# Modulation sums of a two-layer diffusion trunk: 32x32 turns and row sums on VectorE in place of the wide sums and transposes on TensorE

## The chip, the core and the metric

The kernel runs on one core of one Trainium2 chip. The metric is the device time of one execution in microseconds (us), from the first instruction to the last. Every engine has its own in-order instruction queue: TensorE (PE, with its weight loads shown apart as PEld), VectorE (DVE), ScalarE (ACT), GpSimd (POOL) and SyncE (SP, which here only starts transfers). Engines wait for each other through semaphores.

## The reference, cut to what matters

Two layers, each of a SwiGLU FFN, a mixing sub-layer and a second FFN, run on a latent stream `x` and a context stream `h` of 256 tokens with 1024 channels each. Every sub-layer is shifted, scaled and gated by nine vectors of 1024 values for each stream that come from a matrix-vector product. These are the modulation vectors, and they are what the change is about:

```python
sc, scc = silu(c), silu(c_ctx)                       # (1, 1024), (1024,)
for l in range(2):
    mod_x = (sc  @ w_mod[l] + b_mod[l]).reshape(b_, 9, 1, 1024)   # w_mod[l]: 1024 x 9216
    mod_h = (scc @ w_mod[l] + b_mod[l]).reshape(9, 1, 1024)
    # sub-layer j uses mod 3j (shift), 3j+1 (scale), 3j+2 (gate)
    y = rmsnorm(s, norm_pre[l, j]) * (1 + scale) + shift
    s = s + weight * gate * rmsnorm(f(y), norm_post[l, j])
```

`f` is `(silu(y @ wg) * (y @ wu)) @ wd` with 2816 hidden columns for the FFNs, and a mix of gated position mixing and two kinds of attention for the middle sub-layer. All of it is float32.

## The kernel before, in words

**Main work.** Every large product is computed in float32 as three products of split numbers: a weight chunk `stg` that a transfer has landed is split into `hi` (ScalarE, line 240) and `lo` (VectorE, line 101), activations are held as `Yh`/`Yl` (and `Uh`/`Ul` for hidden values), and TensorE adds `hi*Yh`, `hi*Yl` (line 250) and `lo*Yh` (line 254). In the FFN a *pair* is two hidden tiles of 128 columns, each with a gate tile `g` and an up tile `u` of 24 matmuls of 512 columns. After each tile, `hidden` makes the SwiGLU on ScalarE and VectorE (lines 566 to 570 and 101). The `down` part uses lines 263, 269 and 271. Weight chunks pass through three `stg` buffers and three `hi` and three `lo` buffers.

**Modulation vectors.** The first two (layer 0, `q` 0 and 1) are computed at the start on TensorE by `mod_first`. The other 16 are computed by `mod_half`, one half of 512 columns at a time: 32 halves in all. A half loads two weight chunks into the same `stg` buffers, and VectorE multiplies them by the per-partition values of `silu(c)` and `silu(c_ctx)` and adds into two accumulators `acc` (one for each stream, 128x512): 2 instructions on line 355 and 14 on line 357. What is left is the sum over the 128 partitions. After a delay `T_MOD` TensorE does it with a matrix of ones (line 367): four matmuls of 256 columns, each for a quarter of the two streams' values, side by side in four groups of 32 columns of the array.

**What follows the sums.** Of the 16 vectors, 6 are gates (`q % 3 == 2`, 12 halves): VectorE adds the bias and multiplies by the norm gain (lines 375 and 376, tiles `gr` of 128x256, for which `by_groups` loads bias and gain by broadcasts on SP's queue), and POOL's queue stores four rows to the table `gtab` in device memory. The other 10 (20 halves) must end with channels on partitions: ScalarE copies the sums to `modev` (line 383), and at the next sum `flip_now` runs the stored `turn`: two 128x128 transposes on TensorE (line 388) and `mod_put` on VectorE (lines 331 to 334), which writes `coef`.

**What sets the order.** The kernel is written by a small planner: `tick(n)` moves a planned clock by `n` TensorE columns, and generators (`task`, `later`) resume when their planned time has come. `step()` starts a half, at most one in `MOD_PACE` us of the planned clock; `drain` forces what is still pending before a vector is used. In practice one half runs with each pair in the FFNs of both layers except the last. `half(...)` takes one of six buffers of 128x512, `pc()` one of two PSUM banks. The instructions of each engine are then placed in a fixed order, which the order listings below show.

Of the kernel before, what the change touches and what calls it, by code (L numbers as in the profile page):

```python
# [12 lines left out]
F32 = mybir.dt.float32  # L13
F32R = mybir.dt.float32r
AF = mybir.ActivationFunctionType
ALU = mybir.AluOpType
# [3 lines left out]
P = 128  # L20
# [15 lines left out]


T_SOFT, T_SOFTC, T_TURN, T_POST = 4.5, 3.5, 1.5, 3.0
T_MOD, T_FLIP, MOD_PACE = 15.0, 2.5, 18.0
PACE_IN, PACE_OUT, PACE_DRAIN = 1.8, 1.0, 1.0  # L40
PACE_IN1, PACE_OUT1, PACE_DRAIN1, T_CHAIN, T_LATE = 1.5, 1.2, 1.2, 7.5, 10.5
PHASES = ((0, 6), (6, 8), (14, 8))
# [21 lines left out]
def trunk(ctx: ExitStack, tc: tile.TileContext, x, c, cx, c_ctx, w_mod, b_mod, norm_pre, norm_post,  # L64
# [16 lines left out]
    def nm(s):  # L81
        cnt[0] += 1
        return f"{s}{cnt[0]}"
# [7 lines left out]
    def pc():  # L91
        return psc.tile([P, 512], F32, tag="c", name=nm("pc"))

    def half(s):
        return wk.tile([P, 512], F32, tag="p", name=nm(s), bufs=6)
# [24 lines left out]
    def tick(n):  # L120
        clk[0] += n / 2400.0
        while evq and not busy[0] and evq[0][0] <= clk[0]:
            run_next()
# [7 lines left out]

        later(delay, run())

    flips = []

    def flip_now():
        while flips:
            flips.pop(0)()

    def drain(tag):  # L140
        while pending.get(tag, 0):
            run_next()
        if tag[0] == "m":
            flip_now()


    ident = const.tile([P, P], F32, name="ident")
    make_identity(nc, ident)
    ones = const.tile([P, P], F32, name="ones")
    nc.vector.memset(ones, 1.0)  # L150
    negh = const.tile([P, 8], F32, name="negh")
    nc.vector.memset(negh, -0.5)
    mask = const.tile([P, 2, P], F32, name="mask")
# [182 lines left out]


    def by_groups(src):
        r = wk.tile([P, 256], F32, tag="sq", name=nm("gr"), bufs=7)
        for j in range(4):  # L340
            nc.sync.dma_start(r[32 * j:32 * j + 32, :],
                              src[256 * (j % 2):256 * (j % 2) + 256].partition_broadcast(32))
        return r

    def mod_half(l, q, hf):
# [15 lines left out]
        if gate:  # L361
            br = by_groups(b_mod[l, c0:c0 + 512])
            gr = by_groups(norm_post[l, j, hf * 512:(hf + 1) * 512])
        yield T_MOD
        t = pc()
        for i in range(4):
            nc.tensor.matmul(t[32 * i:32 * i + 32, 0:256], lhsT=ones[:, 0:32],
                             rhs=acc[i // 2][:, 256 * (i % 2):256 * (i % 2) + 256],
                             start=True, stop=True, tile_position=(0, 32 * i))
        tick(1024)  # L370
        flip_now()
        if gate:

            w = math.sqrt(D) * (1.0 if j == 1 else 0.5)
            nc.vector.tensor_tensor(br, t[:, 0:256], br, op=ALU.add)
            nc.vector.scalar_tensor_tensor(br, br, w, gr, op0=ALU.mult, op1=ALU.mult)  # L376
            for i in range(4):
                f0 = hf * 512 + 256 * (i % 2)
                nc.gpsimd.dma_start(gtab[l, j][i // 2:i // 2 + 1, f0:f0 + 256],  # L379
                                    br[32 * i:32 * i + 1, :])  # L380
            return
        ev = wk.tile([P, 256], F32, tag="sq", name=nm("modev"), bufs=7)
        nc.scalar.activation(ev, t[:, 0:256], AF.Copy)

        def turn():
            u = pc()
            for i in range(2):
                nc.tensor.transpose(u[:, i * P:(i + 1) * P], ev[:, i * P:(i + 1) * P], ident)
            tick(600)
            uv = u[:, 0:256].rearrange("p (i s h r) -> p h i s r", i=2, s=2, h=2)  # L390
            tmp = sm.tile([P, 2, 2, 2], F32, tag="modt", name=nm("modt"))
            for h in range(2):
                mod_put(l, q, 4 * hf + 2 * h, 2, uv[:, h, :, :, 0], tmp[:, h])

        flips.append(turn)

    modq = []

# [930 lines left out]
```

## Time and profile before

| | |
|---|---|
| median of 3 runs | 1762.75 us (1761.02 to 1763.5) |
| the profiled execution's own time | 1762.98 us |
| its span in the trace | 1761.2 us |
| PE busy | 1722.4 us (98%) |
| PEld busy | 1449.9 us (82%) |
| DVE busy | 1190.4 us (68%) |
| ACT busy | 696.3 us (40%) |
| POOL busy | 168.9 us (10%) |
| TensorE clock granted, mean | 0.997 of full speed |

A matmul's record overlaps the next one's, so the duration of one matmul is not what it costs in a full stream: that is the distance from one start to the next. For VectorE and ScalarE, too, the distance of starts is somewhat shorter than a record's duration. Idle time is printed in brackets behind a row, with the engine that ended it.

### The profile page before, as it was taken

Reading aid. Unit: us, or ns where it says so; the run is one execution under the profiler, and the core shown is the slowest. Engines: PE = TensorE matmul, PEld = TensorE weight load, DVE = VectorE, ACT = ScalarE, POOL = GpSimd, SP = SyncE. Lnnn points to the kernel's source line nnn. Section 1 sums busy time; section 2 is a strip of 40 time slices with the busy share of each in tenths; the row PEclk is TensorE's granted clock in tenths of the full one; section 3 lists DMA queues with packets and bytes.
Section 4 is the critical chain, followed back from the end, with each engine's and each line's share of the span. In section 5 each row is a group of like instructions: output and inputs, shape, how many; then the busy total and the mean of one; then the engine's idle time right before and its main releaser. Section 6 shows DMA issues by size and latency. Waiting matters only on the chain.

```text
span 1761.2 us, 24837 instructions
## 1 busy us (share of the span) xinstructions
PE 1722.4 (98%) x9663; PEld 1449.9 (82%) x9663; DVE 1190.4 (68%) x2174; ACT 696.3 (40%) x1480; POOL 168.9 (10%) x185
## 2 busy tenths in 40 slices
PE   7999999999999999999999999999999999999998
PEld 5788888879977789888888898888888897689997
DVE  4876876775667576768766576777864756765555
ACT  4332322244376562333232442332223526655443
POOL 0000000021322120000000210000001321010000
PEclk9999999999999999999999999999999999999999
DMA  9654554543131143445545233655544133226552
GB/s 336 207 173 160 188 197 144 167 150 109 60 103 52 57 137 125 162 163 189 191 144 185 75 120 123 205 178 191 180 144 167 48 108 120 73 90 197 192 191 84
DMA packets 197105, 259.20 MB, mean 147 GB/s; under 512 B 8234, under 2 KB 132348, under 8 KB 196988
## 3 DMA queue, kind: packets, MB, share of 16 engines
q1 hardware_dynamic: 195452, 257.56, 44.3%
q8 instruction: 76, 1.25, 0.3%
q14 instruction: 41, 0.34, 0.1%
q0 software_dynamic: 1536, 0.05, 0.0%
HBM read 256.49 MB, written 1.10 MB: 146 GB/s over the span
## 4 chain that ended last, share of the span: by engine, by line
PE 63%; DVE 7%; ACT 2%; issue 2%; POOL 1%; DMA 1%; POOLq 0%; DVEq 0%; ACTq 0%
PE pa L250 19%; PE pa L254 9%; PE pb L269 4%; PE pb L271 4%; PE pb L263 4%; PE pa L263 4%; PE pa L271 4%; PE pa L269 4%; PE pb L250 3%; DVE lo L101 2%; PE pb L254 1%; PE pa L797 1%; PE pc L818 1%; PE pc L895 1%; DVE S L439 1%
## 5 line engine op out<-in xcount | busy, mean ns | idle before, releaser
L101 DVE TENSOR_TENSOR lo<-stg,hi 128x512 fp32r<-128x512 f32 (+3 forms) x476 | 367.0, 807 | 192.5 <-ACT hi L240 122.8
L240 ACT ACTIVATE hi<-stg 128x512 fp32r<-128x512 f32 (+3 forms) x496 | 318.4, 702 | 329.6 <-PE pa L263 97.2
L250 PE MATMUL pa<-Yh,hi 128*128 128x512 f32 (+1 forms) x1168 | 415.0, 365 | 0.0
L250 PE MATMUL pa<-Yl,hi 128*128 128x512 f32 (+1 forms) x1168 | 413.8, 364 | 0.0
L357 DVE SCALAR_TENSOR_TENSOR acc<-stg,sT,acc 128x512 f32<-128x512 f32 x448 | 305.2, 743 | 4.0 <-DMA stg<-in_w_mod_dram 4.0
L254 PE MATMUL pa<-Yh,lo 128*128 128x512 f32 (+1 forms) x1168 | 257.8, 363 | 0.0
L250 PEld LDWEIGHTS pa<-Yh,hi 128*128 128x128 f32 x1168 | 220.5, 189 | 36.6 <-issue 2.9
L250 PEld LDWEIGHTS pa<-Yl,hi 128*128 128x128 f32 x1168 | 220.5, 189 | 35.0 <-issue 1.2
L254 PEld LDWEIGHTS pa<-Yh,lo 128*128 128x128 f32 x1168 | 202.4, 189 | 34.3
L570 ACT ACTIVATE Uh<-ha 128x512 fp32r<-128x512 f32 (+1 forms) x92 | 50.7, 551 | 296.4 <-DVE ha L568 296.4
L263 PE MATMUL pb<-hi,Ul 128*128 128x512 f32 x400 | 156.9, 392 | 0.0
L271 PE MATMUL pb<-lo,Uh 128*128 128x512 f32 x400 | 155.9, 390 | 0.8 <-DVE lo L101 0.8
L269 PE MATMUL pb<-hi,Uh 128*128 128x512 f32 x400 | 155.8, 391 | 0.1
L568 DVE TENSOR_TENSOR ha<-ha,pa 128x512 f32<-128x512 f32 (+1 forms) x91 | 53.0, 583 | 79.5 <-PE pa L254 79.0
L269 PE MATMUL pa<-Yh,hi 128*128 128x256 f32 x368 | 92.0, 285 | 0.0
L271 PE MATMUL pa<-Yl,hi 128*128 128x256 f32 x368 | 91.3, 283 | 0.0
L271 PEld LDWEIGHTS pb<-lo,Uh 128*128 128x128 f32 x400 | 75.1, 188 | 16.6 <-DVE lo L101 1.3
L263 PEld LDWEIGHTS pb<-hi,Ul 128*128 128x128 f32 x400 | 75.1, 188 | 16.5 <-issue 1.2
L269 PEld LDWEIGHTS pb<-hi,Uh 128*128 128x128 f32 x400 | 75.2, 188 | 16.0 <-DVE Z L503 0.5
L566 ACT ACTIVATE ht<-pa 128x512 f32<-128x512 f32 (+1 forms) x91 | 46.3, 510 | 104.1 <-PE pa L254 81.8
L379 POOL DMA_DIRECT2D gate<-gr x48 | 24.3, 513 | 603.7 <-DVE gr L376 535.3
L567 DVE SCALAR_TENSOR_TENSOR ha<-ht,pa 128x512 f32<-128x512 f32 (+1 forms) x91 | 52.9, 581 | 37.2 <-ACT ht L566 36.4
(299 smaller groups left out, 2732.4 us busy)
## 6 DMA issues: line engine op xcount, KB each, us to landing
stg<-in_w_mod_dram SPq DMA_DIRECT2D x64, 1024.0 KB, 5.0
stg<-in_ffn_w_gate_dram SPq DMA_DIRECT2D x42, 1024.0 KB, 5.2
stg<-in_ffn_w_up_dram SPq DMA_DIRECT2D x42, 1024.0 KB, 5.1
stg<-in_ffn_w_down_dram SPq DMA_DIRECT2D x32, 1024.0 KB, 5.0
stg<-in_w_in_dram SPq DMA_DIRECT2D x14, 1024.0 KB, 4.8
stg<-in_ffn_w_down_dram SPq DMA_DIRECT2D x16, 768.0 KB, 4.4
mst<-in_w_mod_dram SPq DMA_DIRECT2D x16, 512.0 KB, 7.6
stg<-in_w_out_dram SPq DMA_DIRECT2D x8, 1024.0 KB, 6.4
```

The costliest lines, as they stand in the source:

```text
L101: eng.tensor_tensor(lo, full, f32(hi), op=ALU.subtract)
L240: nc.scalar.activation(hi[:, a:b, :], v[:, a:b, :], AF.Copy)
L250: nc.tensor.matmul(o, lhsT=ah, rhs=r, start=(i == 0), stop=(i == n - 1))
L254: nc.tensor.matmul(o, lhsT=al, rhs=bh, start=(i == 0), stop=(i == n - 1))
L263: nc.tensor.matmul(o, lhsT=al, rhs=bh, start=False, stop=last, skip_group_check=True)
L269: nc.tensor.matmul(o, lhsT=ah, rhs=bh, start=(first and k == 0), stop=False, skip_group_check=True)
L271: nc.tensor.matmul(o, lhsT=ah, rhs=bl, start=False, stop=False, skip_group_check=True)
L357: nc.vector.scalar_tensor_tensor(a, v[:, k, :], sc, a, op0=ALU.mult, op1=ALU.add)
L566: nc.scalar.activation(t, g, AF.Tanh, scale=0.5)
L567: nc.vector.scalar_tensor_tensor(a, t, 1.0, g, op0=ALU.add, op1=ALU.mult)
L568: nc.vector.tensor_tensor(a, a, u, op=ALU.mult)
L570: nc.scalar.activation(uh, a, AF.Copy)
```

## The change

1. VectorE gets four new instructions in each half, right behind the products: for each stream a turn of every 32x32 block of `acc` (into a buffer `mt` from `half`) and a sum over each group of 32 along the row, into `sums` (128 x 2 x 16). After that each value is left as four partial sums on four groups of 32 partitions.
2. TensorE adds the four: for a gate with one matmul of 32 columns (`sums` as weights, the selector `sel` as moving data), otherwise with four matmuls of 8 columns in the four column groups (`sel` as weights), whose result already has channels on partitions. The wide sums with `ones`, the ScalarE copy `modev`, the two transposes and the `flips` list go. `mod_put` runs once for 4 blocks and not twice for 2.
3. `by_groups` loads bias and gain into 32x32 tiles (two loads each, not four broadcasts, from a pool of 4 buffers), and a gate's table is stored by two transfers and not four.
4. `T_MOD` goes from 15 to 17, `MOD_PACE` from 18 to 17.5, and the planned clock moves by 600 columns at a sum (before 1024, and 600 at a flip).

```diff
-T_MOD, T_FLIP, MOD_PACE = 15.0, 2.5, 18.0
+T_MOD, T_FLIP, MOD_PACE = 17.0, 2.5, 17.5
...
-    ones = const.tile([P, P], F32, name="ones")
-    nc.vector.memset(ones, 1.0)
+    sel = const.tile([P, 32], F32, name="sel")
+    nc.vector.tensor_reduce(sel, ident.rearrange("p (g j) -> p j g", g=4), axis=AX.X, op=ALU.add)
...
     def by_groups(src):
-        r = wk.tile([P, 256], F32, tag="sq", name=nm("gr"), bufs=7)
-        for j in range(4):
-            nc.sync.dma_start(r[32 * j:32 * j + 32, :],
-                              src[256 * (j % 2):256 * (j % 2) + 256].partition_broadcast(32))
+        r = sm.tile([32, 32], F32, tag="gr", name=nm("gr"))
+        for st in range(2):
+            nc.sync.dma_start(r[16 * st:16 * st + 16, :], src.rearrange("(b c) -> b c", c=32))
...
+        sums = sm.tile([P, 2, 16], F32, tag="sums", name=nm("sums"))
+        for st, a in enumerate(acc):
+            turned = half("mt")
+            nc.vector.transpose(turned, a)
+            nc.vector.tensor_reduce(sums[:, st, :], turned.rearrange("p (b i) -> p b i", i=32), axis=AX.X,
+                                    op=ALU.add)
         yield T_MOD
         t = pc()
-        for i in range(4):
-            nc.tensor.matmul(t[32 * i:32 * i + 32, 0:256], lhsT=ones[:, 0:32],
-                             rhs=acc[i // 2][:, 256 * (i % 2):256 * (i % 2) + 256],
-                             start=True, stop=True, tile_position=(0, 32 * i))
-        tick(1024)
-        flip_now()
         if gate:
+            nc.tensor.matmul(t[0:32, 0:32], lhsT=sums.rearrange("p s b -> p (s b)"), rhs=sel,
+                             start=True, stop=True)
+            tick(600)
...
-        ev = wk.tile([P, 256], F32, tag="sq", name=nm("modev"), bufs=7)
-        nc.scalar.activation(ev, t[:, 0:256], AF.Copy)
-        def turn():
-            u = pc()
-            for i in range(2):
-                nc.tensor.transpose(u[:, i * P:(i + 1) * P], ev[:, i * P:(i + 1) * P], ident)
...
+        sv = sums.rearrange("p s (b m) -> p s b m", m=4)
+        for m in range(4):
+            nc.tensor.matmul(t[32 * m:32 * m + 32, 0:8], lhsT=sel, rhs=sv[:, :, :, m], start=True,
+                             stop=True, tile_position=(0, 32 * m))
+        tick(600)
+        tmp = sm.tile([P, 4, 2], F32, tag="modt4", name=nm("modt"))
+        mod_put(l, q, 4 * hf, 4, t[:, 0:8].rearrange("p (s b) -> p b s", s=2), tmp)
```

**Where the instructions stand now.** First TensorE, in the second phase of the first FFN, at the sum of a half that is not a gate. In the first listing (before) the sum stands between the gate tile and the up tile of a pair, with the flip of the half ahead behind it:

```order
L254 MATMUL pa210_1554<-Yh_102,lo197_1454 128x512 x8
L367 MATMUL pc211_1579<-acc202_1477,ones_89 32x256 x2
L367 MATMUL pc211_1579<-acc203_1478,ones_89 32x256 x2
L388 MATMUL pc212_1584<-ident_84,modev190_1417 128x128 x2
L250 MATMUL pa215_1592<-Yh_102,hi199_1465 128x512
```

The same place in the changed kernel:

```order
L243 MATMUL pa224_1590<-Yh_102,hi209_1469 128x512
L243 MATMUL pa224_1590<-Yl_103,hi209_1469 128x512
L243 MATMUL pa224_1590<-Yh_102,hi209_1469 128x512
L379 MATMUL pc225_1600<-sums216_1503,sel_89 32x8 x4
L243 MATMUL pa224_1590<-Yl_103,hi209_1469 128x512
```

Four matmuls of 256 columns and two transposes are replaced by four matmuls of 8 columns, nine matmuls later in the stream.

Then VectorE at the first half, early in the first FFN. Before, the last product is followed at once by the SwiGLU of tile 3 (`ha_719`) and the splits of the next pair's gate weights (`lo_728`) and up weights (`lo_740`):

```order
L357 SCALAR_TENSOR_TENSOR acc_640<-stg_651,sT,acc_640 128x512
L567 SCALAR_TENSOR_TENSOR ha_719<-ht_718,pa_623 128x512
L101 TENSOR_TENSOR lo_728<-stg_725,hi_727 128x512 x3
L568 TENSOR_TENSOR ha_719<-ha_719,pa_624 128x512
L101 TENSOR_TENSOR lo_728<-stg_725,hi_727 128x512
L101 TENSOR_TENSOR lo_740<-stg_737,hi_739 128x512
L101 TENSOR_TENSOR Ul_601<-ha_719,Uh_600 128x512
L101 TENSOR_TENSOR lo_740<-stg_737,hi_739 128x512 x3
```

The same place in the changed kernel (there `ha_722`, `lo_731`, `lo_743`):

```order
L349 SCALAR_TENSOR_TENSOR acc_640<-stg_651,sT,acc_640 128x512
L360 STREAM_TRANSPOSE mt_668<-acc_639 128x512
L360 STREAM_TRANSPOSE mt_671<-acc_640 128x512
L361 TENSOR_REDUCE sums_667<-mt_668 128x16
L361 TENSOR_REDUCE sums_667<-mt_671 128x16
L555 SCALAR_TENSOR_TENSOR ha_722<-ht_721,pa_623 128x512
L101 TENSOR_TENSOR lo_731<-stg_728,hi_730 128x512
L556 TENSOR_TENSOR ha_722<-ha_722,pa_624 128x512
L101 TENSOR_TENSOR lo_731<-stg_728,hi_730 128x512 x2
L101 TENSOR_TENSOR Ul_601<-ha_722,Uh_600 128x512
L101 TENSOR_TENSOR lo_731<-stg_728,hi_730 128x512
L101 TENSOR_TENSOR lo_743<-stg_740,hi_742 128x512 x4
```

Four instructions stand ahead of the splits now, and the last quarter of the gate weights' split has moved behind `Ul`.

Last SP, behind the weight loads of the second half, in the changed kernel. The loads of bias and gain for the third gate half (`gr_1847`, `gr_1850`) stand here, ahead of two weight chunks; before, they stood 24 rows further down:

```order
L205 DMA stg_894<-in_w_mod_dram 128x4x512
L205 DMA stg_904<-in_w_mod_dram 128x4x512
L334 DMA gr_1847<-in_b_mod_dram 16x32 x2
L334 DMA gr_1850<-in_norm_post_dram 16x32 x2
L205 DMA stg_1003<-in_ffn_w_down_dram 128x3x512
```

With four buffers and two tiles to a gate half, these loads need the buffers of the first gate half back.

## Rows read from the trace of the kernel before

**Rows 1.** The page, busy time: engine, us (share of the span) x instructions.

```profile
PE 1722.4 (98%) x9663; PEld 1449.9 (82%) x9663; DVE 1190.4 (68%) x2174; ACT 696.3 (40%) x1480; POOL 168.9 (10%) x185
```

**Rows 2.** Busy by stretch: length; PE, PEld, DVE, ACT, POOL (count); clock, DMA share, GB/s.

```profile
55.00:97.00 42.00, 42.00 (x191) 34.23 (x190) 40.45 (x69) 15.82 (x27) 2.43 (x4) 1.00 0.64 203
...
500.00:640.00 140.00, 134.02 (x852) 107.34 (x851) 94.82 (x247) 87.06 (x250) 28.68 (x23) 1.00 0.21 72
...
738.00:837.00 99.00, 99.00 (x460) 79.78 (x459) 74.81 (x125) 33.28 (x59) 0.00 (x0) 1.00 0.55 181
```

**Rows 3.** TensorE in order of time, a sum with a flip: start, us, engine, operation.

```profile
802.68 1.98 PE L254 MATMUL pa<-Yh,lo 128*128 128x512 f32 x8
...
808.12 1.98 PE L254 MATMUL pa<-Yh,lo 128*128 128x512 f32 x8
810.03 0.64 PE L367 MATMUL pc<-acc,ones 128*32 128x256 f32 x8
810.60 0.44 PE L388 MATMUL pc<-ident,modev 128*128 128x128 f32 x2
...
814.53 1.98 PE L254 MATMUL pa<-Yh,lo 128*128 128x512 f32 x8
```

**Rows 4.** TensorE in order of time, the first gate's sum, without a flip.

```profile
78.35 1.97 PE L254 MATMUL pa<-Yh,lo 128*128 128x512 f32 x8
80.25 0.64 PE L367 MATMUL pc<-acc,ones 128*32 128x256 f32 x8
...
84.59 1.98 PE L254 MATMUL pa<-Yh,lo 128*128 128x512 f32 x8
```

**Rows 5.** How many: line 367 by its source, line 388 by its form.

```profile
L367 PE MATMUL pc<-acc,ones x256: 376/379/404, 80.3 to 1322.7; 128*32 128x256 f32 x128
```

```profile
L388 PE MATMUL pc<-ident,modev 128*128 128x128 f32 x40 | 8.6, 296 | 0.0
```

**Rows 6.** TensorE in order of time, other small float32 matmuls, in the mixing part.

```profile
604.22 0.66 PE L929 MATMUL pc<-wsT,VG 128*64 128x128 f32 x8
604.80 0.50 PE L269 MATMUL pb<-hi,Yh 128*128 128x512 f32 x1
...
607.95 0.44 PE L929 MATMUL pc<-wsT,VG 128*64 128x128 f32 x4
608.32 0.50 PE L263 MATMUL pb<-hi,Yl 128*128 128x512 f32 x1
```

**Rows 7.** The chain that ended last, 128-column weights with 64 columns: start, us.

```profile
590.80 1.93 PE pc L895 x16
```

**Rows 8.** VectorE by form: count | busy us, mean ns | idle before.

```profile
L101 DVE TENSOR_TENSOR lo<-stg,hi 128x1024 fp32r<-128x1024 f32 x87 | 106.7, 1240 | 31.4 <-PE pa L254 16.9 <-ACT hi L240 14.3 <-ACT hi L235 0.2
...
L800 DVE TENSOR_REDUCE mx<-pa 128x1 f32<-128x512 f32 x32 | 21.4, 684 | 3.2 <-PE pa L797 3.0
...
L704 DVE STREAM_SHUFFLE shf<-QK 128x256 f32<-128x256 f32 x16 | 6.4, 447 | 0.0
```

**Rows 9.** VectorE in order of time, one steady pair, idle time in brackets.

```profile
787.46 1.29 DVE L101 TENSOR_TENSOR lo<-stg,hi 128x512 fp32r<-128x512 f32 x2 [3.42 <-PE pa L254]
...
806.26 0.69 DVE L101 TENSOR_TENSOR Ul<-ha,Uh 128x512 fp32r<-128x512 f32 x1 [0.70 <-ACT Uh L570]
810.19 1.29 DVE L101 TENSOR_TENSOR lo<-stg,hi 128x512 fp32r<-128x512 f32 x2 [3.24 <-PE pa L254]
```

**Rows 10.** VectorE in order of time, the end of the first half.

```profile
67.17 5.38 DVE L357 SCALAR_TENSOR_TENSOR acc<-stg,sT,acc 128x512 f32<-128x512 f32 x8
...
73.07 1.88 DVE L101 TENSOR_TENSOR lo<-stg,hi 128x512 fp32r<-128x512 f32 x3
...
75.53 1.29 DVE L101 TENSOR_TENSOR lo<-stg,hi 128x512 fp32r<-128x512 f32 x2
```

**Rows 11.** Transfer issues: SP's in order of time, and POOL's gate stores (us to landing).

```profile
90.57 4.39 SPq L212 DMA_DIRECT2D stg<-in_ffn_w_down_dram  x2
```

```profile
gate<-gr POOLq DMA_DIRECT2D x48, 1.0 KB, 2.2
```

More of the change, by code (lines that the diff above doesn't have):

```diff
@@ L132, in task @@
         later(delay, run())
[L134 to L138, printed above, removed]
     def drain(tag):
@@ L142, in drain @@
             run_next()
-        if tag[0] == "m":
-            flip_now()
     ident = const.tile([P, P], F32, name="ident")
     make_identity(nc, ident)
-    ones = const.tile([P, P], F32, name="ones")
-    nc.vector.memset(ones, 1.0)
+    sel = const.tile([P, 32], F32, name="sel")
+    nc.vector.tensor_reduce(sel, ident.rearrange("p (g j) -> p j g", g=4), axis=AX.X, op=ALU.add)
     negh = const.tile([P, 8], F32, name="negh")
@@ L370, in mod_half @@
-        tick(1024)
-        flip_now()
         if gate:
+            nc.tensor.matmul(t[0:32, 0:32], lhsT=sums.rearrange("p s b -> p (s b)"), rhs=sel,
+                             start=True, stop=True)
+            tick(600)
             w = math.sqrt(D) * (1.0 if j == 1 else 0.5)
-            nc.vector.tensor_tensor(br, t[:, 0:256], br, op=ALU.add)
+            nc.vector.tensor_tensor(br, t[0:32, 0:32], br, op=ALU.add)
             nc.vector.scalar_tensor_tensor(br, br, w, gr, op0=ALU.mult, op1=ALU.mult)
[L377 to L380, printed above, removed]
+            for st in range(2):
+                nc.gpsimd.dma_start(gtab[l, j][st, hf * 512:(hf + 1) * 512]
+                                    .rearrange("(b c) -> b c", c=32), br[16 * st:16 * st + 16, :])
@@ L381, in mod_half @@
             return
-        ev = wk.tile([P, 256], F32, tag="sq", name=nm("modev"), bufs=7)
-        nc.scalar.activation(ev, t[:, 0:256], AF.Copy)
-        def turn():
-            u = pc()
-            for i in range(2):
-                nc.tensor.transpose(u[:, i * P:(i + 1) * P], ev[:, i * P:(i + 1) * P], ident)
[L389 to L393, printed above, removed]
@@ L395, in mod_half @@
-        flips.append(turn)
+        sv = sums.rearrange("p s (b m) -> p s b m", m=4)
[5 more added lines that the diff above has]
+        mod_put(l, q, 4 * hf, 4, t[:, 0:8].rearrange("p (s b) -> p b s", s=2), tmp)
     modq = []
```

## Prediction

> **What bounds the kernel now.** I read the page's busy times first [rows 1]: PE is busy for 98% of the span, far ahead of DVE's 68%. But an average hides stages, so I read the busy time by stretch next [rows 2]. Where modulation halves run, in the FFNs, PE is busy for the whole stretch (42.00 of 42.00 us, 99.00 of 99.00), with all of the clock granted; in the attention stretch, where no half runs, it is idle for 6.0 of 140 us. A busy PE could still be badly used, so the third view is TensorE in order of time [rows 3]: the eight matmuls with `lo` start 5.44 us apart from one tile to the next (802.68, 808.12), which is 24 matmuls at 0.227 us, a stream without a hole. There, whatever is taken out of TensorE's queue comes straight off the end time, as long as nobody is late for it. DVE is the engine that could be late: in the steady stretch it is busy for 74.81 of 99 us, at the start of the first FFN for 40.45 of 42 [rows 2].
>
> **What leaves TensorE.** The tile that holds a sum and a flip takes 814.53 - 808.12 = 6.41 us, 0.97 more than 5.44 [rows 3]. With a sum alone it takes 84.59 - 78.35 = 6.24, so 0.80 more [rows 4]; a flip costs 0.17. Of the 0.80, 0.57 lie between the sum's start and the next start (810.03, 810.60) [rows 3]; the other 0.23 are a late start and a slow restart of the stream around it. The 256 records of line 367 are 128 matmuls in two passes, so 32 sums of four; the 40 of line 388 are 20 flips of two transposes [rows 5]. All sums together cost 32 x 0.80 + 20 x 0.17 = 29.0 us.
>
> **What comes in on TensorE.** The new matmuls are float32 and use 32-column groups of the array, like the old. The trace has none with 8 columns, so I bound them. For a floor I use line 929, small float32 matmuls in column groups, too: 8 records of 128 columns hold the stream for 604.80 - 604.22 = 0.58 us, 4 records for 608.32 - 607.95 = 0.37 [rows 6]. The second four cost 0.21, so 0.37 - 0.21 = 0.16 does not depend on the columns; line 367's 0.57 less 0.16 is 0.41 for 256 columns, and 8 columns at that rate are 0.01: floor 0.17. For a ceiling I use line 895: 16 records with full 128-column weights in 1.93 us, 0.12 each [rows 7]; four matmuls are 8 records, 0.97. I take 0.25 for the four and 0.19 for a gate's single one: the row with the same column groups is nearer than one that loads four times the weights, and I add 0.08 and 0.02 for starts that so few columns cannot hide. The 0.23 around the block stay, since the stream is still broken once a half. For a half that is no gate the sum is then 0.23 + 0.25 = 0.48 in place of 0.97, for a gate 0.23 + 0.19 = 0.42 in place of 0.80. **Saved: 20 x 0.49 + 12 x 0.38 = 9.8 + 4.6 = 14.4 us.** At the floor it would be 20 x 0.57 + 12 x 0.40 = 16.2; at the ceiling (0.97 and 0.24) 20 x -0.23 + 12 x 0.33 = -0.6, a small loss.
>
> On this the Trainium skill has a rule that speaks against shrinking the columns (page "TensorEngine Tiling (Array Packing)", section "Instruction Overhead"): every matmul carries about 60 cycles, so one with a single column takes as long as one with 60. By that rule, at line 367's 0.41 us for 256 columns, 60 columns are an estimated 0.10 us, the block 0.26, and the sum 14.2 us where mine is 14.4; no run here has shown a matmul this small. The same page ("Key Properties") says that a change of tiling mode drains the engine, which agrees with the 0.23 that I leave in place.
>
> **What comes in on DVE, and why I cost it at nothing.** Each half gets two 128x512 turns and two 128x512 row sums. A row sum of that size takes 0.68 us (line 800). A turn is not in the trace; the nearest row is the 32-lane shuffle, 0.45 us for 256 columns (line 704), so about 0.7 for 512, and I bound it by the 1.24 of an instruction of twice the size (line 101) [rows 8]. Starts lie closer than durations (8 products in 5.38 us, 0.67 apart [rows 10]), so I take 4 x 0.65 = 2.6 us a half, at the bound 3.8. Leaving DVE are two 128x256 instructions of a gate or half of the small `mod_put` instructions, some tenths, which I don't count. The cover is DVE's idle time: in a steady pair of 810.19 - 787.46 = 22.73 us it idles 0.70 + 3.24 = 3.94 us [rows 9]. 2.6 fit, and 3.8 just fit. Without that cover each us would cost a us a half.
>
> At the start of the first FFN there is no such idle time. Products end at 67.17 + 5.38 = 72.55 and the splits of `lo` follow from 73.07 [rows 10]; the first use is TensorE's eight matmuls from 78.35, the last quarter of the weights from the seventh of them, 79.71 [rows 4]. In the new order 2.6 us of turns and sums, then `ha`, a split, `ha`, two splits, `Ul` and the last split follow, seven at 0.60: 72.5 + 2.6 + 4.2 = 79.3. Slack 0.4 us; at the 3.8 bound it misses by 0.8, once. Further back, DVE's backlog shrinks, since `acc` is free when the turns have read it and no longer waits for TensorE.
>
> TensorE's own wait grows by the four instructions: `sums` of the first half are there at 72.5 + 2.6 = 75.1. The old sum ran at 80.25 [rows 4], the new one stands nine matmuls later, at about 82: 7 us of slack, and in order behind it stands the whole stream, so a miss would cost all of itself. It doesn't miss.
>
> **Queues and ACT.** The `modev` copy leaves ACT, which is not the bound (40%) [rows 1]. On SP the loads `gr` of the third gate half now stand ahead of two weight chunks and need the first gate half's buffers back, so they wait for POOL's store: sum at 82, two small DVE instructions, two issues, 2.2 us to landing [rows 11], done by about 88. The chunk behind them was issued only at 90.57 [rows 11], as it waits for its own buffer. Cost nothing, with 2.5 us of cover; beyond that, each us makes a weight chunk late. Later gate halves have a pair of 22.7 us between them.
>
> **The rivals.** (a) *The tiny matmuls are bound by their number, not their columns*: 0.12 a record as in [rows 7]; against it stands that line 367 runs 8 records in 0.57. It gives 1762.98 + 0.6 = 1763.6, no change. Chance 0.07. (b) *DVE becomes the engine that ends last*: above 3.94 us a half, TensorE waits for `ha` or `lo`, and above 3.94 + 0.45 (saved a half) the kernel is slower. That needs turns of over 1.5 us each. At 2.5 us a turn, a half adds 2 x 2.5 + 1.3 = 6.3, so 2.4 over, 32 x 2.4 = 75 us, less 14: about 1824. No row of 512 columns is near that. Chance 0.05. (c) *Part of the gain is given back*: a miss at the first pair, a late chunk, or the mixing part, whose order moves a little since the planned clock moves less at a sum and a flip there is gone; PE already idles 6 us there [rows 2]. 1751 to 1757, chance 0.17. (d) *The floor holds and TensorE's small waits go, too*: 16.2 to 18 us saved, 1745 to 1746.8, chance 0.08.
>
> **How the numbers follow.** The profiled execution took 1762.98 us (span 1761.2), 0.23 above the median of the runs, 1762.75. 1762.98 - 14.4 = 1748.6, and 1748.4 against the median: I say 1748.5. My own forecast, 1747 to 1751, has chance 0.63. Range 1745 to 1756: it takes in (d), the forecast and most of (c), and leaves out (a), (b) and the end of (c). A measurement of this kernel can tell about 0.2%, 3.5 us, from no change. Faster: 0.63 + 0.17 + 0.08 = 0.88; same 0.07; slower 0.05.
>
> **What would show it.** Right: the tile with a sum takes about 5.44 + 0.48 us, PE's busy time falls by some 14 us with idle time as before, DVE's rises by some 75 us, turns are near 0.7 us, and no wait of TensorE for `sums` or `lo` is new in the FFNs. Wrong: a new matmul block near 1 us; idle time on TensorE that ends with `lo`, `ha` or `sums`; DVE without idle time in steady pairs; SP waiting for a gate's store while a weight chunk is due.

## The result, and the profile after

The changed kernel takes 1744.29 us (median of 4 runs, 1743.18 to 1744.91), the kernel before 1763.03 in the same comparison: a ratio of 0.9897, 95% interval 0.9884 to 0.991. It is 18.7 us faster, where 14.4 were forecast; the direction is right, and the time lies 0.7 us below the low end of the range. Ratios below are to the kernel before in the same comparison, with their 95% interval.

The page of the changed kernel begins like this (busy us, share of the span, instructions of each engine); beside it stand [rows 1]:

```profile
span 1743.1 us, 24539 instructions
PE 1708.0 (98%) x9551; PEld 1448.2 (83%) x9551; DVE 1257.9 (72%) x2272; ACT 689.8 (40%) x1460; POOL 156.0 (9%) x161
```

TensorE's busy time fell from 1722.4 to 1708.0, which is 14.4 us, as forecast. That agreement is partly chance: busy time is made of durations that overlap, and by starts, below, the sums saved 16.2. The span fell by 18.1, so TensorE's idle time fell too, from 38.8 to 35.1 us. VectorE's busy time rose by 67.5 us (some 75 forecast). The same stretches as in [rows 2], busy us of each engine, then granted clock:

```profile
738.00:837.00 99.00, 99.00 (x463) 80.98 (x462) 92.80 (x151) 30.74 (x51) 0.00 (x0) 1.00 0.58 189
500.00:640.00 140.00, 135.09 (x835) 108.22 (x834) 91.59 (x235) 84.51 (x238) 28.94 (x23) 0.98 0.18 56
```

In the steady stretch VectorE is now busy for 92.80 of 99 us (74.81 before), and TensorE still has no hole. In the attention stretch the granted clock is 0.98, which it was not before; that comes back below.

TensorE in order of time, one sum of a half that is no gate, in the steady stretch (start, duration; to be read against [rows 3]):

```profile
777.38 1.98 PE L247 MATMUL pa<-Yh,lo 128*128 128x512 f32 x8
...
781.01 0.39 PE L243 MATMUL pa<-Yh,hi 128*128 128x512 f32 x1
781.33 0.25 PE L379 MATMUL pc<-sums,sel 128*32 128x8 f32 x8
781.50 0.50 PE L243 MATMUL pa<-Yl,hi 128*128 128x512 f32 x1
781.84 0.39 PE L243 MATMUL pa<-Yh,hi 128*128 128x512 f32 x1
...
783.23 1.98 PE L247 MATMUL pa<-Yh,lo 128*128 128x512 f32 x8
```

The tile takes 783.23 - 777.38 = 5.85 us, 0.41 more than 5.44. Inside, the block starts 0.32 after the matmul ahead of it (0.227 is normal), the next matmul 0.17 after the block, the one behind that 0.34 later. And the first gate's single matmul (against [rows 4]):

```profile
80.89 0.39 PE L243 MATMUL pa<-Yh,hi 128*128 128x512 f32 x1
81.21 0.25 PE L366 MATMUL pc<-sel,sums 128*32 128x32 f32 x2
81.39 0.50 PE L243 MATMUL pa<-Yl,hi 128*128 128x512 f32 x1
81.72 0.39 PE L243 MATMUL pa<-Yh,hi 128*128 128x512 f32 x1
```

Its block is 0.18. One matmul of 32 columns and four of 8 cost the same; the median over all sums of this trace is 0.18 for both. What is around the block, 0.23, stayed as the prediction left it.

VectorE's new instructions, grouped by line (xcount, busy us, mean ns):

```profile
L360 DVE STREAM_TRANSPOSE mt<-acc 128x512 f32<-128x512 f32 x64 | 41.8, 687 | 0.0
L361 DVE TENSOR_REDUCE sums<-mt 128x16 f32<-128x512 f32 x64 | 39.9, 658 | 0.0
```

A turn of 512 columns takes 0.69 us and a row sum 0.66, 0.65 and 0.62 from start to start.

**Where the 18.1 us of span come from.** I laid the two traces over each other, the start of the same matmul in both, and read by how much the changed kernel is ahead. After 26 us it is 1.2 us ahead: the kernel before ran its first large matmuls (20.9 to 24.2 us) at a granted clock of 0.50, which is 1.2 GHz, the changed one at 1.00, 2.4 GHz. Eleven halves of the first FFN bring it to 6.5. That FFN's last down part, with the twelfth half, adds 2.9 (9.4), where a sum and a lone flip account for about 0.8; the other 2 us need a reason. The first attention takes 2.6 back (6.8; first and second attention are those of the first and the second layer). Ten halves of the second FFN lead to 12.0, its end to 13.1, ten halves of the third to 17.7; the last matmul starts 17.5 earlier, and the kernel ends 18.1 earlier. So the sums gave 20 x (0.97 - 0.40) + 12 x (0.80 - 0.40) = 16.2 us, and some 2 us net came from elsewhere.

That net is a sum of gains and losses, and only two of them belong to the change: the 2 us of the down part, and 0.6 us behind the last matmul. From its end to the end of the kernel it is 7.3 us in the changed kernel and 8.0 in the one before. Every other trace made from the one has 7.3 to 7.4, from the other 8.0 to 8.2; x11 alone has 10.2. What differs there is the DRAIN instruction with which GpSimd's queue closes (queue, count, then shortest, median and longest in ns; the longest one counts); before, then after, then x11:

```profile
L1325 POOLq DRAIN  x3: 102/182/4905, 1755.1 to 1760.8; - x3
L1313 POOLq DRAIN  x3: 34/93/2937, 1737.6 to 1742.8; - x3
L1339 POOLq DRAIN  x3: 40/102/7523, 1725.3 to 1733.3; - x3
```

GpSimd starts 48, 24 and 80 transfers in these three, so each adds about 0.08 us to this instruction. x8, with 12 transfers and 1.96 us, ends no earlier behind its last matmul than the changed kernel: the closing counts only where it ends last, as in the kernel before and in x11. That it makes the whole 0.6 is argued from these traces; no run tests it alone. The other parts of the net come and go between executions: the start's clock (1.2 gained), the first attention (2.6 lost, below), and a wait of TensorE for VectorE's `Z` at the end of the second FFN, 0.8 shorter here:

```profile
1033.13 0.99 PE L461 MATMUL pb<-ident,Z 128*128 128x128 f32 x7 [1.41 <-DVE Z L447]
1020.06 0.98 PE L449 MATMUL pb<-ident,Z 128*128 128x128 f32 x7 [0.61 <-DVE Z L435]
```

x2, whose TensorE instructions stand in the order of the changed kernel's, waits 1.46 us there, so this 0.8 can't be credited to the change.

### The profile page after: what moved, and what is told of

Its sections match the earlier page's. It is cut to its first block, busy times and chain, and to the rows that moved or that the text cites. A ratio compares the mean times of both kernels' runs of the same rounds, so it can differ in the third digit from the quotient of the medians.

```text
span 1743.1 us, 24539 instructions
## 1 busy us (share of the span) xinstructions
PE 1708.0 (98%) x9551; PEld 1448.2 (83%) x9551; DVE 1257.9 (72%) x2272; ACT 689.8 (40%) x1460; POOL 156.0 (9%) x161
## 4 chain that ended last, share of the span: by engine, by line
PE 86%; DVE 7%; ACT 3%; issue 2%; POOL 1%; DMA 1%; POOLq 0%; DVEq 0%; ACTq 0%; SPq 0%
PE pa L243 27%; PE pa L247 13%; PE pb L262 6%; PE pb L256 6%; PE pb L264 6%; PE pa L256 5%; PE pa L264 5%; PE pa L262 5%; PE pb L243 3%; DVE lo L101 2%; PE pb L247 2%; PE pa L1242 1%; PE pa L785 1%; PE pc L806 1%; PE pc L883 1%
## 5 line engine op out<-in xcount | busy, mean ns | idle before, releaser
L243 PEld LDWEIGHTS pa<-Yl,hi 128*128 128x128 f32 x1168 | 220.5, 189 | 34.5
L243 PEld LDWEIGHTS pa<-Yh,hi 128*128 128x128 f32 x1168 | 220.5, 189 | 33.7
L264 PEld LDWEIGHTS pa<-Yl,hi 128*128 128x128 f32 x368 | 70.6, 192 | 0.1
L262 PEld LDWEIGHTS pa<-Yh,hi 128*128 128x128 f32 x368 | 70.5, 192 | 0.1
```

Source lines behind the costliest of these rows:

```text
L243: nc.tensor.matmul(o, lhsT=ah, rhs=r, start=(i == 0), stop=(i == n - 1))
L262: nc.tensor.matmul(o, lhsT=ah, rhs=bh, start=(first and k == 0), stop=False, skip_group_check=True)
L264: nc.tensor.matmul(o, lhsT=ah, rhs=bl, start=False, stop=False, skip_group_check=True)
```

## The experiments

Two questions were open: why a block costs what it costs, and where the 2 us outside the sums come from. Times are compared with 1744.3 for the changed kernel and 1763 for the one before. A matter of 1 or 2 us has to be read with the run's granted clock, since a kernel's own runs scatter with it: the kernel before took 1759.8 to 1761.8 us at a mean clock of 0.999 and 1762.8 to 1765.2 at 0.996 in these comparisons.

### x1: every small matmul four times

```diff
+            for _ in range(4):
                 nc.tensor.matmul(t[0:32, 0:32], lhsT=sums..., rhs=sel, ...
...
-        for m in range(4):
+        for m in (0, 1, 2, 3) * 4:
             nc.tensor.matmul(t[32 * m:32 * m + 32, 0:8], lhsT=sel, ...
```

> Every sum's matmuls are issued four times (16 of 8 columns for a half that is no gate, 4 of 32 columns for a gate), results unchanged. The changed kernel's block of four stands 0.17 us from start to next start, its single gate matmul 0.18. Theory 'fixed block': the 0.17 is the price of entering and leaving, and what is inside counts by columns alone (0.41 us for 256 columns of the old sum, 0.0016 each): 128 columns in four groups in place of 32 add 24 columns a group, 0.04; a gate's 96 more columns 0.15. 20 x 0.04 + 12 x 0.15 = 2.6, 1746.9 us. Theory 'a start costs 0.02' (what the prediction added to the floor): 12 x 0.02 = 0.24 a half, 3 x 0.02 a gate on top of the columns: 1746.9 + 5.5 = 1752.4 us. Theory 'by number', 0.12 a record: 24 records more, 2.9 us a half, over 1800 us.

Measured: 1748.4 us (0.9923, 0.9903 to 0.9943). TensorE in x1 at a gate's sum, and at that of a half that is none (start, duration):

```profile
81.33 0.44 PE L367 MATMUL pc<-sel,sums 128*32 128x32 f32 x8
81.70 0.50 PE L243 MATMUL pa<-Yl,hi 128*128 128x512 f32 x1
...
170.15 0.44 PE L380 MATMUL pc<-sums,sel 128*32 128x8 f32 x32
170.52 0.50 PE L243 MATMUL pa<-Yl,hi 128*128 128x512 f32 x1
```

Both blocks are 0.37. Three more matmuls of 32 columns in one group cost 0.19; twelve more of 8 columns in four groups, three in each, cost 0.20. So a small matmul costs about 0.065 us in its own group, whether it has 8 or 32 columns, and the four groups run side by side. "By columns alone" (0.04 for the half) falls, "0.02 for each start" (0.28 with the columns) is nearer but counts the groups one after the other, and "by number at 0.12 a record" is far off. The trace has 20 x 0.20 + 12 x 0.19 = 6.3 us more in the sums; the span is only 3.5 longer (1746.6), because this run did not meet the slow stretch of the first attention.

### x2: 64 columns in place of 8

```diff
-            nc.tensor.matmul(t[32 * m:32 * m + 32, 0:8], lhsT=sel, rhs=sv[:, :, :, m], ...
+            nc.tensor.matmul(t[32 * m:32 * m + 32, 0:64], lhsT=sel,
+                             rhs=sT.rearrange("p k c -> p (k c)")[:, 64 * m:64 * m + 64], ...
```

> The four matmuls of a half that is no gate have 64 columns in place of 8; they read 64 columns of a constant tile in place of the sums, so shift and scale come out wrong. Theory 'fixed block plus columns': 56 x 0.0016 = 0.09 more, block 0.26, 20 x 0.09 = 1.8, 1746.1 us. Rival 'the first some 60 columns are free because each matmul has a least time': block stays 0.17, 1744.3 us.

Measured: 1744.9 us (0.9903, 0.9884 to 0.9923). TensorE in x2 at such a sum:

```profile
169.41 0.32 PE L379 MATMUL pc<-sT,sel 128*32 128x64 f32 x8
169.66 0.50 PE L243 MATMUL pa<-Yl,hi 128*128 128x512 f32 x1
```

The block is 0.25, so 56 columns cost 0.08: "fixed block plus columns" has it right on the trace (the time alone, 1.2 us from the one theory and 0.6 from the other, could not have told). In x1 a further matmul in the same group cost the same with 8 columns as with 32; but four of 16 cost 0.01 to 0.03 more than four of 8 (x8, below). How many columns are free, if any, is not shown. The rule of the Trainium skill (page "TensorEngine Tiling (Array Packing)", section "Instruction Overhead"), by which a matmul of 1 column takes as long as one of 60, agrees in kind with x1's 8 and 32 columns and does not hold here for 8 against 64: at line 367's 0.0016 us a column, the four columns beyond 60 would be an estimated 0.01 us, where 0.08 was measured.

### x3: the same sums on the whole array

```diff
+    selz = const.tile([P, 224], F32, name="selz")
...
-            nc.tensor.matmul(t[32 * m:32 * m + 32, 0:8], lhsT=sel, rhs=sv[:, :, :, m], ...
+            nc.tensor.matmul(t[:, 0:8], lhsT=selz[:, 96 - 32 * m:224 - 32 * m], rhs=sv[:, :, :, m],
+                             start=(m == 0), stop=(m == 3))
```

> The four matmuls of a half that is no gate use 128-column weights (the selection padded with zeros) and add up in one place, in place of four 32-column groups of the array; the same sums come out. A sum now costs 0.40 us: a block of 0.17 and 0.23 for a late start and a slow restart of the stream around it. Theory 'the 0.23 is the change to column groups': it goes, and the block grows by its wider weights; with 0.12 a record (8 records) it is 0.97 at most, so a sum costs 0.17 to 0.97, 1740 to 1756 us, and the starts before and after the block are 0.23 apart. Theory 'the 0.23 is the change from one float type to the other': the starts around stay late (0.32 and 0.33), 1744 us or more.

Measured: 1751.85 us (0.9943, 0.9923 to 0.9963). TensorE in x3 around one sum:

```profile
169.64 0.40 PE L245 MATMUL pa<-Yh,hi 128*128 128x512 f32 x1
169.87 0.96 PE L381 MATMUL pc<-sums,selz 128*128 128x8 f32 x8
170.69 0.47 PE L245 MATMUL pa<-Yl,hi 128*128 128x512 f32 x1
171.00 0.39 PE L245 MATMUL pa<-Yh,hi 128*128 128x512 f32 x1
```

Eight records with 128-column weights take 0.82, 0.10 each: the ceiling of the prediction (0.12 from [rows 7], 0.97 for the block) describes these, not column groups. The block starts 0.23 after its neighbour, so the late start (0.09) belongs to entering the column groups; the restart of 0.31 stays slow, so that part (0.09) does not. Both theories were half right. A sum in this form costs 0.82 + 0.09 = 0.91 in place of 0.41. That is 20 x 0.5 = 10 us in all; the time is only 7.6 longer, since this run, like x1's, did not meet the slow stretch of the first attention.

### x4: the sums without TensorE

```diff
-            nc.tensor.matmul(t[0:32, 0:32], lhsT=sums..., rhs=sel, ...
...
-        for m in range(4):
-            nc.tensor.matmul(t[32 * m:32 * m + 32, 0:8], lhsT=sel, rhs=sv[:, :, :, m], ...
```

> The matmuls that add the four partial sums are left out (shift, scale and gate are made from one partial sum, so the output is wrong); VectorE's turns and row sums stay. Theory 'a sum costs TensorE 0.40 us and nothing else': 32 x 0.40 = 12.8 less than the changed kernel, 1731.5 us. Rival 'what TensorE saves comes back as waits for VectorE' (it has 1.4 us of idle time a pair left): 1735 to 1744 us, with new idle time ended by lo or ha.

Measured: 1730.6 us (ratio to the kernel before 0.9823, 0.9807 to 0.984), 13.7 less than the changed kernel, in another comparison. That it is so near the 12.8 is partly luck: this run did not meet the slow stretch of the first attention (2.8 us) and lost 0.9 to the wait for `Z` and another 0.6 in and behind the second attention. Laid over the changed kernel's trace, the halves of the three FFNs gain 4.68, 4.06 and 4.07 us, 12.8 together. So the theory holds: 0.40 a half, and TensorE has no new wait for `lo`, `ha` or `sums`.

### x5 and x6: the planner's numbers, alone

```diff
-T_MOD, T_FLIP, MOD_PACE = 17.0, 2.5, 17.5
+T_MOD, T_FLIP, MOD_PACE = 15.0, 2.5, 18.0
...
-            tick(600)
+            tick(1024)
...
-        tick(600)
+        tick(1024)
```

> The changed kernel with the planner's numbers of before (a half's sum due 15.0 after its start and not 17.0, pace 18.0 and not 17.5, 1024 columns booked for a sum and not 600). The order then puts each sum nine matmuls earlier, where the kernel before has it; the twelfth sum of the first FFN stays near the 74th matmul of the last down part (26th in the kernel before, 83rd in the changed one). Theory 'the gain outside the sums comes from acc, which the turns free early': the stall of 2.0 us in that down part stays away; a sum 7 us after its data stays without a wait; 1744 us, or 1741.5 if the stretch of 1.2 GHz in the first attention (2.9 us) is not met. Theory 'it comes from the planner's numbers': the stall is back, 1746 us, with TensorE idle until lo near 363 us.

Measured: 1742.3 us (0.989, 0.9871 to 0.9909). At a clock of 0.996 it is 1744.44, where the changed kernel has 1743.18 and 1744.48. The stall stayed away. x6 puts 17.0 and 17.5 into the kernel before and changes nothing else:

> The kernel before with the planner's numbers of the changed one (17.0 and 17.5), nothing else. Theory 'acc': the stall until lo in the first FFN's last down part stays, since the twelfth sum stays at the 26th matmul; 1763 us within 2. Theory 'planner': the stall goes, and with it about 2 us or more: 1761 us or less.

Measured: 1765.9 us (1.0016, 1.0007 to 1.0026), and TensorE waits for acc for 1.07 us at the twelfth sum and for lo behind it. The planner's numbers are not the reason. In the kernel before they cost 0.7 us at that wait; the rest of the 2.9 us to the kernel before may be the clock, since seven of its ten runs had a mean of 0.994 or 0.995.

### x7 and x9: when acc comes free

```diff
         sums = sm.tile([P, 2, 16], F32, tag="sums", name=nm("sums"))
+        yield T_MOD - 4.0
         ...
-        yield T_MOD
+        yield 4.0
```

> The changed kernel, but VectorE turns and sums a half's rows only 13.0 of the planner's us after the products are issued in the program, 4.0 before the matmul is due, so that acc is freed late again, as in the kernel before; the matmuls stand where they stood. Theory 'acc': VectorE's products of the next half wait for acc again, its work bunches up, TensorE waits for lo, ha or sums once or more: 2 to 4 us longer, 1746 to 1748 us. Theory 'acc plays no part': 1744 us, no new wait of TensorE.

Measured: 1742.6 us (0.9891, 0.9876 to 0.9906), no new wait of TensorE. x9 takes the kernel before, and acc from other buffers:

```diff
-        acc = [wk.tile([P, 512], F32, tag="a", name=nm("acc")) for _ in range(2)]
+        acc = [half("acc") for _ in range(2)]
```

> The kernel before with one edit: acc comes from the six buffers that ht and ha use, and not from the two of its own, so that VectorE can begin the products of a half while TensorE has yet to read those of the one before. Nothing else is changed, the sums stand where they stood. Theory 'the stall of 2.0 us in the first FFN's last down part comes from products that wait for acc': TensorE's waits until acc and lo at 363 to 365 us go, 1761 us, and VectorE's idle time that ends with TensorE's L367 (30.4 us in 9 waits) goes too. Rival 'VectorE is simply full there': the waits stay, 1763 us. Third case: ha and ht miss the buffers and TensorE gets new waits, over 1763 us.

Measured: 1762.8 us (1.0002, 0.9992 to 1.0012). What VectorE sat idle for ahead of a half's first products (line 355) in the kernel before, in us, times, is by far the most of it TensorE's sum:

```profile
  PE pc L367: 30.4, 9
```

In x9 this line is gone, and TensorE's stall in the last down part is not:

```profile
362.27 1.20 PE L367 MATMUL pc<-acc,ones 128*32 128x256 f32 x8 [0.63 <-DVE acc L357]
364.25 0.50 PE L271 MATMUL pb<-lo,Uh 128*128 128x512 f32 x1 [0.78 <-DVE lo L101]
```

My theory fell: without the 30 us of VectorE's waits the kernel is no faster, and the stall has another cause.

### x12: the flip that started a half

In the kernel before, the last flip ahead of a final down part moves the planner's clock, and that starts what has fallen due: the twelfth half, ahead of the down part's own weights. The change has no flips, so the half starts behind the first of them.

```diff
         if tag[0] == "m":
+            busy[0] = True
             flip_now()
+            busy[0] = False
```

> The kernel before with one edit: a flip that is made when a layer's modulation is waited for (ahead of the last down part) books its columns on the planner's clock, but no longer starts what has fallen due there. In the kernel before that flip starts the twelfth half of the first FFN, ahead of the last down part's own weights: its products come on VectorE in front of those weights' splits, and its sum stands at the 26th matmul of the down part. With the edit the half starts behind the first of the weights and its sum stands at the 74th matmul, where the changed kernel (which has no flips) has it at the 83rd. Theory 'the 2.0 us outside the sums come from this place in the order': TensorE's waits until acc and lo at 363 to 365 us go, the kernel takes 1761 us where the one before takes 1763 (2 us within the scatter of the first attention's clock, so the trace decides). Rival 'VectorE is full there whatever the order': the waits stay or come elsewhere in 340 to 380 us.

TensorE at this place in the kernel before, and then in x12:

```profile
362.48 0.39 PE L269 MATMUL pb<-hi,Uh 128*128 128x512 f32 x1
363.25 1.20 PE L367 MATMUL pc<-acc,ones 128*32 128x256 f32 x8 [0.38 <-DVE acc L357]
365.22 0.50 PE L271 MATMUL pb<-lo,Uh 128*128 128x512 f32 x1 [0.78 <-DVE lo L101]
```

```profile
362.59 0.39 PE L273 MATMUL pb<-lo,Uh 128*128 128x512 f32 x1
...
373.24 0.50 PE L273 MATMUL pb<-Yl,Uh 128*128 128x512 f32 x1 [0.58 <-DVE Yl L101]
...
375.05 0.64 PE L369 MATMUL pc<-acc,ones 128*32 128x256 f32 x8
```

The waits for acc and lo are gone, and behind that place the kernel is 2.6 us ahead of the one before; a new wait of 0.58 and the sum, which now comes later, take 1.8 of it back. About 0.9 us of the 2 are left on the trace. The time is 1762.55 us (0.9995, 0.9986 to 1.0004), not to be told from the kernel before; at the same mean clock its runs are a little shorter (0.998: 1760.7 us in the mean where all runs of the kernel before have 1761.3; 0.996: 1763.0 and 1763.8). So the place in the order is shown to be the cause of the stall and of about 0.9 us. Of the other 1.1 us, x12's own new wait for `Yl` makes up most: it puts 0.98 us between two starts (372.26 to 373.24) where 0.23 is normal. The changed kernel has no such wait, and its twelfth sum stands in the stream like any other:

```profile
369.01 0.25 PE L379 MATMUL pc<-sums,sel 128*32 128x8 f32 x8
```

Why `Yl` is in time there and not in x12 stays open.

### x10: twice the work on VectorE

```diff
             nc.vector.transpose(turned, a)
             nc.vector.tensor_reduce(sums[:, st, :], ...
+            nc.vector.transpose(turned, a)
+            nc.vector.tensor_reduce(sums[:, st, :], ...
```

> Every turn and every row sum is done twice, the output is unchanged: 128 instructions of 0.65 and 0.62 between starts more, 2.54 us a half, 81 us in all on VectorE. In the changed kernel VectorE is idle for 6.2 us of the steady 99 (92.80 busy), 1.39 us a pair. Theory 'a pair must cover its own half': 2.54 - 1.39 = 1.15 us are late in each of some 20 halves in steady pairs, 1744 + 23 = 1767 us, with TensorE idle until ha or lo. Rival 'VectorE may run behind and catch up where no half runs' (it is idle for 47 us of 325 in the first FFN, 64 of 280 in the second, so 12 x 2.54 and 10 x 2.54 fit): 1744 to 1749 us.

Measured: 1744.35 us (0.9892, 0.9875 to 0.9908), the same as the changed kernel. VectorE's busy time on its page and its steady stretch:

```profile
PE 1705.6 (98%) x9551; PEld 1446.9 (83%) x9551; DVE 1333.5 (77%) x2400; ACT 690.1 (40%) x1460; POOL 156.8 (9%) x161
738.00:837.00 99.00, 99.00 (x464) 80.99 (x463) 95.47 (x156) 29.15 (x48) 0.00 (x0) 1.00 0.53 181
```

76 us more of VectorE's time cost next to nothing. Laid over the changed kernel's trace, x10 loses 0.5 us in the first FFN's last down part (a wait of 0.24 for `Yl` that the changed kernel does not have) and nothing in the other FFNs; that its time is the same is also due to the first attention, whose slow stretch it did not meet. The steady stretch holds only 2.7 of the 76 us, where 4.4 pairs with 2.54 each would be 11: VectorE falls behind and makes it up where no half runs (behind the first FFN's halves, from 325 to 400 us, it is busy for 63.74 us in place of 54.90). "A pair must cover its own half" falls.

### x8: two halves in one block

```diff
-        sums = sm.tile([P, 2, 16], F32, tag="sums", name=nm("sums"))
+        if not hf:
+            both_sums[l, q] = sm.tile([P, 2, 2, 16], F32, tag="sums", name=nm("sums"))
+        sums = both_sums[l, q]
...
+        if not hf:
+            return
         yield T_MOD
...
-            nc.tensor.matmul(t[32 * m:32 * m + 32, 0:8], ...
+            nc.tensor.matmul(t[32 * m:32 * m + 32, 0:16], ...
```

> A version meant to be better: the partial sums of two halves of one vector are added in one block (four matmuls of 16 columns, or one of 64 by 32 for a gate), at the second half's place; 16 blocks in place of 32. Theory 'a block costs 0.40 us whatever few columns it has': 16 x 0.40 = 6.4 less, 1737.9 us. Theory 'what is inside counts': a block of twice the columns costs up to 0.07 more (64 columns in place of 8 are on record with 0.25 in place of 0.17), 16 x 0.33 = 5.3 less, 1739 us. Rival 'the late sum is waited for': TensorE idle until sums, 1742 us or more.

Measured: 1741.5 us (0.9878, 0.9859 to 0.9898). TensorE in x8 at a gate's block and at one for shift or scale:

```profile
114.33 0.30 PE L372 MATMUL pc<-sel,sums 128*64 128x32 f32 x2
114.56 0.50 PE L256 MATMUL pb<-hi,Ul 128*128 128x512 f32 x1
...
168.73 0.26 PE L385 MATMUL pc<-sums,sel 128*32 128x16 f32 x8
168.93 0.50 PE L243 MATMUL pa<-Yl,hi 128*128 128x512 f32 x1
```

The blocks are 0.23 and 0.20 (0.19 in the median of ten), and by 1280 us the version is 5.8 us ahead of the changed kernel, as expected. Behind that it loses some 2.5 us: 0.9 at the end of the third FFN, where TensorE waits 1.17 us for `Z` (0.28 in the changed kernel) at a granted clock of 1.00, and 1.6 in the second attention, where its clock is 0.50 for 6.8 us (3.4 in the changed kernel). Its runs had a mean clock of 0.994 for three of four, and the fourth, at 0.999, took 1737.1 us.

### x11: the sums by transfers

```diff
+        nc.gpsimd.dma_start(box.rearrange("m p c -> p m c"), sums.rearrange("p (m c) -> p m c", m=4))
...
+        yield 6.0
...
+            for m in range(4):
+                nc.gpsimd.dma_start(r[32 * m:32 * m + 32],
+                                    box.rearrange("m (g j) c -> m j g c", g=4)[m])
+        yield T_MOD - 6.0
...
-            nc.tensor.matmul(t[32 * m:32 * m + 32, 0:8], lhsT=sel, ...
+        nc.vector.tensor_reduce(t, r.rearrange("p g c -> p c g"), axis=AX.X, op=ALU.add)
```

> A version meant to be better still, without any matmul for the sums: the partial sums of two halves go to memory and come back side by side by GpSimd's transfers (1 and 4 for shift and scale, 1 and 2 for a gate), and VectorE adds the four in one small instruction. Theory 'TensorE's 0.40 a half is all that the sums cost': 12.8 less than the changed kernel, 1731.5 us, as with the matmuls left out. Rival 'GpSimd's issues or the way through memory come late': TensorE waits in the last down parts or VectorE waits for the data with splits queued behind, 1735 us or more.

Measured: 1733.95 us, the fastest of all that computes the whole (0.9834, 0.982 to 0.9849; 10.3 us below the changed kernel, in another comparison). On VectorE the small instruction waits for the transfer (busy us, mean ns, then idle us before it):

```profile
L406 DVE TENSOR_REDUCE mq<-mr 128x16 f32<-128x64 f32 x10 | 2.7, 266 | 29.3 <-DMA mr<-sumd 29.3
L395 DVE TENSOR_REDUCE mq<-mr 64x32 f32<-64x128 f32 x6 | 2.2, 373 | 11.5 <-DMA mr<-sumd 11.5
```

40.8 us of waiting on VectorE, and no new wait of TensorE: the rival's wait is there and costs nothing. At 0.996 its runs took 1732.0 and 1732.6. Laid over the changed kernel's trace, its halves gain what x4's do, within 0.1 us in each FFN. In the profiled run 0.8 are lost to a longer wait for `Z`, and 2.8 behind the last matmul, where GpSimd closes its 80 transfers for 7.5 us: that is the price of this way, and a version that starts fewer transfers from GpSimd was not run.

## Where the prediction was right, and where it was not

**What bounds the kernel.** Right: x4 took the sums' TensorE time out, and the whole of it, 12.8 us, came off the halves.

**The block on TensorE.** The floor, 0.17, was the true size, and so 16.2 us were saved where 14.4 were summed; the step that failed is the 0.08 and 0.02 added to it "for starts that so few columns cannot hide". x1 shows such a price for small matmuls (0.065 each in a group), but four that start in four groups run side by side, and the first of each lies within the fixed 0.17. Measured 0.17 and 0.18, with the 0.23 around them 0.40 to 0.41 where 0.48 and 0.42 were taken. This is 20 x 0.08 + 12 x 0.02 = 1.8 us of the 4.3 that were missed. The 0.23 itself was right; x3 splits it into 0.09 for entering the column groups and the slow restart, whose cause stays open.

**Idle time as before.** This step failed too. The prediction looked for waits that the change could add and left those that it could remove to rival (d), with at most 1.8 us. The wait of TensorE for acc and lo in the first FFN's last down part was on record in the trace of before, 1.16 us together, and was not costed; with what stands around it, it gave 2 us of the 4.3. Another 0.6 came at the end of the kernel, where GpSimd closes 24 transfers in place of 48: the prediction gave the two stores in place of four no price. The other gains and losses (1.2 and 0.8 won, 2.6 lost, and some tenths) can't be credited to the change and add up to a loss of less than 1 us: that so little of them was left is luck. The reason for the wait could not be read from the diff's numbers: a flip's small booking on the planner's clock decided which of two loads came first (x12), and neither the planner's numbers (x5, x6) nor the release of acc (x7, x9) did.

**VectorE at no cost.** Right in the result: turns of 0.69 where 0.7 was taken, row sums of 0.66 where 0.68 was. Wrong in the reason: the cover was said to be a pair's own 3.94 us, and x10 shows that another 2.5 us a half cost 0.5 us in all, so rival (b) was further off than its price of 3.94 us a half made it.

**First pair, queues.** No wait of TensorE for lo, ha or sums came at the first pair, and the loads of gr that wait for the gate's store were issued at 86.87 us, ahead of the weight chunk (93.32, it was 90.57 in [rows 11]); TensorE waited for neither.

**The rivals.** (d) is what happened: floor and fewer waits, 16.2 and a net of 1.9 on the trace. Its chance of 0.08 was too small, and the range's low end, 1745, was set by its largest saving, 18 us, which was too small by 0.7. (c) happened in part: the mixing part, which was named, gave 2.6 us back, but through the clock. TensorE in the first attention of the changed kernel, then of x1, from the same instructions:

```profile
575.16 1.44 PE L806 MATMUL pc<-VG,pT 128*128 128x128 f32 x8 [0.98 <-ACT pT L771]
576.52 2.07 PE L853 MATMUL pa<-CU 64*128 64x512 f32 x2
578.53 1.97 PE L769 MATMUL pa<-ident,p 128*128 128x128 f32 x8
580.15 0.78 PE L256 MATMUL pb<-hi,Yl 128*128 128x512 f32 x1
...
582.79 0.39 PE L256 MATMUL pb<-hi,Yl 128*128 128x512 f32 x1
```

```profile
577.61 1.16 PE L807 MATMUL pc<-VG,pT 128*128 128x128 f32 x8 [0.98 <-ACT pT L772]
578.70 1.12 PE L854 MATMUL pa<-CU 64*128 64x512 f32 x2
579.75 1.09 PE L770 MATMUL pa<-ident,p 128*128 128x128 f32 x8
580.60 0.48 PE L256 MATMUL pb<-hi,Yl 128*128 128x512 f32 x1
...
582.07 0.39 PE L256 MATMUL pb<-hi,Yl 128*128 128x512 f32 x1
```

From the first row to the last it is 7.63 us in the one and 4.46 in the other; the first ran at a granted clock of 0.50 (1.2 GHz) until some 582.5, the other at 1.00, after waits of TensorE of some tenths to one us, which both have. Why the clock fell in the one and not in the other is not shown. At the same mean clock, 0.996, the changed kernel took 1743.2 and 1744.5 us and the one before 1762.8 to 1765.2 in the later comparisons: without the clock's share the gain is, as an estimate, 19 to 20 us rather than 18.7.

## What to carry to other kernels

When one engine is busy from end to end, a block of small matmuls in column groups costs it the break in its stream and little else, so make fewer breaks (two sums in one block) or none (another engine, a transfer that the busy engine does not wait for) before you make the blocks smaller. Before you forecast a change that moves work, list the waits that the bounding engine has now and ask of each whether the new order keeps it: waits that go are as real as waits that come. Gains of 2 us in 1760 can't be told from the time alone where the clock changes from run to run; lay the traces over each other at the same instructions.

## What the runs showed of the hardware

- Small float32 matmuls in 32-column groups: block 0.18 us for four of 8 columns and for one of 32, 0.19 for four of 16, 0.25 for four of 64 (medians of all sums in a trace); each further one in the same group 0.065, with 8 or with 32 columns (x1). With 128-column weights it is 0.10 a record and 0.82 for the same four (x3).
- Entering the column groups delays the block by 0.09 us; on the whole array there is no such delay, but the stream restarts slowly (0.31 to 0.34 in place of 0.23) in both.
- Stretches of TensorE at 1.2 GHz at the start and in or behind the two attentions come in some executions and not in others of nearly the same instructions; one in the first attention costs some 3 us (the changed kernel against x1). At the end every trace has one, but it begins behind the last matmul and costs nothing, though the mean clock counts it.
- The DRAIN with which GpSimd's queue closes took 1.96, 2.94, 4.91 and 7.52 us after 12, 24, 48 and 80 transfers (x8, the changed kernel, the one before, x11), about 0.08 us for each.
- VectorE turned 32x32 blocks of 128x512 float32 in 0.69 us, the time of its row sum (0.66), with 76 us of doubled work hidden behind TensorE but for 0.5 us (x10).
